# Gating step of an SSD stage on another engine, its stores on another queue, and other numbers of tile places

## The chip, the cores and the metric

The kernel runs on one core of a Trainium2 chip. A core has five engines that each work through their own list of instructions in order and meet through semaphores: TensorE (PE, matrix products), VectorE (DVE), ScalarE (ACT), GpSimd (POOL) and SyncE (SP, which here issues nearly all DMAs). The metric is the time of one execution on the device, in microseconds, and the figure for a kernel is the median of several executions.

## What is computed

The reference is an encoder trunk of two layers over 1024 tokens of width 1024. The even layer feeds two head groups from one input projection: A is a bidirectional state-space scan (SSD) with an output gate, B is a short gated convolution. The odd layer has latent attention and a multi-scale pooling. Cut to what the change touches:

```python
proj = x @ w_in
z, xbc, dt_raw, sc_bg, sc_cg, sc_h, sc_gate = split(proj)
xbc = silu(depthwise_conv(xbc, conv_w) + conv_b)
xs, bm, cm = split(xbc)
y_a = ssd_bidirectional(xs, bm, cm, dt_raw, a_log, dt_bias, d_skip)   # 16 heads, 4 groups, chunks of 128
y_a = rms_norm(y_a * silu(z), norm_g)
y_b = sc_bg * depthwise_conv(sc_cg * sc_h, sc_conv_w) * silu(sc_gate)
h = concatenate([y_a, y_b]) @ w_out
x = layer_norm(ALPHA * x + h)
```

The line that matters is `y_a * silu(z)`: the scan's output times the gate, whose squares are also summed for the norm.

## The kernel before

All products in float32 are made of three or six passes over pairs of a high and a low part. Layer 0 (`layer0_main`) runs in stages: a front stage projects x, B and C and convolves them (to about 230 us of the profile), the SSD stage computes the scan (about 230 to 600 us), a back stage finishes branch B and starts the output projection (from 600 us on); layer 1 follows.

The SSD stage loops over four groups of heads. For each group it runs over eight chunks twice. In the first pass, `op_p2` takes a chunk's x and B by TensorE transposes to `xps`, ScalarE copies x out (L743), a high and low part of B are made (`bhl`), x is scaled by dt into `xd` (VectorE, L751) and split into `xdh` (ScalarE) and `xdl` (GpSimd); `op_p2s` makes the chunk's state `sps` and adds it to the running states. For groups 1 to 3, `op_z` between them computes the gate's projection `zps` by 24 matmuls a chunk. ScalarE makes `zt`, a tanh (L724), and VectorE the gate `zs` from both (L725); only then is the `zps` place free. `zps` comes from a PSUM pool of two places, which it shares with `gps`, the products of branch B. In the trace `zs` is called ssd.

In the second pass, `op_p3f` loads `E`, decay rows of 512 KB spread over the partitions (L804), and works on them with ScalarE (L809, L810, L813) and VectorE (L811, L816 to L818); `op_p3b` makes the state part `yo` and the diagonal part in `cbp` (L836) on TensorE, moves yo out as `to` (VectorE, L834), adds up in `ta` on GpSimd (L838, L840) and VectorE (L841), multiplies by the gate into `yg` (L843), squares it on ScalarE with a sum into the norm (L844; the square's output overwrites `ta`) and stores `yg` to memory as yad (L845). At the end of a group `op_xl` loads the next group's four x, B and C tiles (L619).

The order of the program is that of `main_plan`: it also deals steps of branch B's products (`gps`) between the chunks, so that TensorE has other work. A scheduler of the framework then sets each engine's order within that. Tiles come from pools; tiles of one tag share a number of places, and a new tile waits until the last reader of the tile that stood in its place is done, a store included. Tag t1 (256 columns, four places) holds `bhl`, `hm`, `zt`, `ta` and `yg`. Tag t2 (512 columns, six places) holds the x tiles `xd`, `xdh`, `xdl` and also `to`. Tag cv (three places after the front stage) holds `brt` of branch B and in the back stage tiles of its Strassen-like combinations (L921, L997, L1002, L1004). `E` has four places.

Of the kernel before, what the change touches and what calls it, by code (L numbers as in the profile page):

```python
# [9 lines left out]
F32 = mybir.dt.float32  # L10
# [3 lines left out]
ALU = mybir.AluOpType  # L14
# [4 lines left out]
P = 128  # L19
# [52 lines left out]
YB_AT = (0, 1, 2, 3, 4, 5, 6, 7)  # L72
X_AT = (10, 11, 12, 13)
WOB, WOI, WOG, PI, NV, LA = 2, 3, 1, 1, 0, 2
T4B, T2B, CVB, RAWB, E2B = 1, 6, 3, 3, 4


def main_plan():
# [175 lines left out]
def bc_last(ap, n):  # L254
    s = list(ap.shape)
    return ap.unsqueeze(len(s)).broadcast_to(s + [n])
# [81 lines left out]
def view(t, n):  # L338
    return t.rearrange("p (a b) -> p a b", a=n)
# [166 lines left out]
def layer0_main(k):  # L506
    nc, tc, a = k.nc, k.tc, k.a
    V, A, GP, PE = nc.vector, nc.scalar, nc.gpsimd, nc.tensor
# [60 lines left out]
    tp = eb4 = dw4 = ecs4 = et4 = dt4 = ed4 = None  # L569
# [56 lines left out]
    def t2(name, dt=F32):  # L626
        return tp.tile([P, 512], dt, name=name, tag="t2", bufs=T2B)
# [2 lines left out]
        return (fp or cvp).tile([P, 512], F32, name=name, tag="cv", bufs=2 if fp is not None else CVB)  # L630

    def t1(name, dt=F32):
        return tp.tile([P, 256], dt, name=name, tag="t1", bufs=4)

    groups = [dict() for _ in range(G)]

# [79 lines left out]
    def op_z(g, c):  # L716
        st = groups[g]
        h, o = c // 4, (c % 4) * P
        ps = k.pa.tile([P, 1024], F32, name="zps", tag="pa")[:, 0:256]
        for kk in range(KD):  # L720
            wh, wl = st["zw"][kk // 4]
            mm3(nc, ps, *(t[:, o:o + P] for t in xhl(h, kk)), view(wh, 4)[:, kk % 4, :], view(wl, 4)[:, kk % 4, :], kk == 0, kk == KD - 1)
        zt = t1("zt")
        A.activation(out=zt, in_=ps, func=AF.Tanh, scale=0.5)  # L724
        V.scalar_tensor_tensor(out=st["zs"][:, c, :], in0=zt, scalar=1.0, in1=ps, op0=ALU.add, op1=ALU.mult)  # L725
# [4 lines left out]
    def h_cols(c):  # L730
        return slice(256 if c == 0 else 0, 256 if c == NB - 1 else 512)

    def dirs(cols):
        return slice(cols.start // 256, cols.stop // 256)

    def op_p2(g, c):
        st = groups[g]
        g4 = slice(4 * g, 4 * g + 4)
        hin = st["hin"]
        ps = k.pb.tile([P, 512], F32, name="xps", tag="pb")  # L740
        for j in range(3):
            st["xp"] = PE.transpose(out=ps[:, P * j:P * j + P], in_=st["xfm"][j][:, P * c:P * c + P], identity=k.ident).ins
        A.copy(out=st["xtm"][:, c, :], in_=ps[:, 0:256])  # L743
        bhl = t1("bhl", F32R)
        bh, bl = bhl[:, 0:P], bhl[:, P:256]
        split(nc, bh, bl, ps[:, 256:384], V)
        xd = t2("xd")
        xv = view(ps[:, 0:256], HPG)
        cols = s_cols(c)
        d = dirs(cols)  # L750
        V.tensor_tensor(out=xd.rearrange("p (q h d) -> p q h d", q=2, h=HPG)[:, d], in0=bc_mid(xv, 1, d.stop - d.start), in1=bc_last(dw4[:, c, d, g4], HD), op=ALU.mult)  # L751
        xh, xl = t2("xdh", F32R), t2("xdl", F32R)
        st["xa", c] = split(nc, xh[:, cols], xl[:, cols], xd[:, cols], nc.gpsimd)
        st["s", c] = (bh, bl, xh[:, cols], xl[:, cols])
# [23 lines left out]
    def h_decay(g, c, d):  # L778
        o = 256 * d
        hm = t1("hm")  # L780
        GP.tensor_tensor(out=view(hm, HPG), in0=view(groups[g]["hin"][:, c, o:o + 256], HPG), in1=bc_last(et4[:, c, d, 4 * g:4 * g + 4], HD), op=ALU.mult)
        return hm
# [39 lines left out]
    def op_p3b(g, c):  # L822
        st = groups[g]
        M, yd = st.pop(("f", c))
        g4 = slice(4 * g, 4 * g + 4)
        blk = slice(P * c, P * c + P)
        xt = st["xtm"][:, c, :]
        yo = k.pb.tile([P, 512], F32, name="yo", tag="pb")
        cols = h_cols(c)
        d = dirs(cols)  # L830
        PE.matmul(yo[:, cols], st["xfm"][3][:, blk], st["hin"][:, c, cols], start=True, stop=True)
        to = t2("to")
        tov, yov = (t.rearrange("p (d h e) -> p d h e", d=2, h=HPG)[:, d] for t in (to, yo))
        V.tensor_tensor(out=tov, in0=yov, in1=bc_last(ecs4[:, c, d, g4], HD), op=ALU.mult)  # L834
        for h in range(HPG):
            st["yd"] = PE.matmul(yd[:, HD * h:HD * h + HD], M[:, P * h:P * h + P], xt[:, HD * h:HD * h + HD], start=True, stop=True).ins  # L836
        ta = t1("ta")
        GP.tensor_tensor(out=view(ta, HPG), in0=view(xt, HPG), in1=bc_last(st.pop(("cd", c)), HD), op=ALU.mult)  # L838
        for q in range(d.start, d.stop):
            GP.tensor_tensor(out=ta, in0=to[:, 256 * q:256 * q + 256], in1=ta, op=ALU.add)  # L840
        V.tensor_tensor(out=ta, in0=yd, in1=ta, op=ALU.add)  # L841
        yg = t1("yg")
        GP.tensor_tensor(out=yg, in0=ta, in1=st["zs"][:, c, :], op=ALU.mult)  # L843
        A.activation(out=ta, in_=yg, func=AF.Square, accum_out=k.ssq[:, c, g:g + 1])  # L844
        nc.sync.dma_start(out=k.yad[c, :, 256 * g:256 * g + 256], in_=yg)  # L845

    def op_end():
        r = k.const.tile([P, NB], F32, name="rinv")
# [169 lines left out]
    def op_ya(c):  # L1018
# [10 lines left out]
        split(nc, t[:, 0, :, o:o + P], t[:, 1, :, o:o + P], view(y, KD), V)  # L1029

    table = {"fm": op_fm, "hold": op_hold, "dt2": op_dt2, "zx": op_zx, "ssd": op_ssd, "xl": op_xl, "z0": op_z0, "z": op_z, "p2": op_p2, "p2s": op_p2s, "p2b": op_p2b, "p3f": op_p3f, "p3b": op_p3b, "dt": op_dt, "end": op_end, "ya": op_ya, "tp": op_tp, "sw": op_sw, "sp": op_sp}
    for op in main_plan():
        table[op[0]](*op[1:])
# [606 lines left out]
```

## Time and profile before

| what | value |
| --- | --- |
| median of three runs (lowest to highest) | 1454.23 us (1453.46 to 1458.45) |
| the profiled execution | 1449.7 us |
| its span, first to last instruction | 1447.9 us |
| mean granted clock of TensorE | 0.983 |
| busy: TensorE, VectorE, ScalarE, GpSimd | 1391.6, 921.2, 692.1, 467.6 us |
| DMA, mean rate over the span | 101 GB/s |

Busy time is time in which an engine carries out an instruction; issuing a DMA or waiting doesn't count. A view of windows gives the same for a stretch of the span, with the clock that TensorE was granted as a share of its full speed (1.00 is 2.4 GHz, 0.50 is 1.2 GHz). A view of waits adds up the idle time of an engine before its instructions by what released it. A timeline lists instructions with their start, their length and, in brackets, the idle time before them and its releaser. A view of a tile lists all instructions that read or write it.

### The profile page before, as it was taken

What the parts mean: (1) busy time and instruction counts of PE and PEld (TensorE: products, weight loads), DVE (VectorE), ACT (ScalarE), POOL (GpSimd) and SP (SyncE); (2) the same over time, 40 slices, a digit from 0 to 9 for tenths busy, and PEclk for the clock granted to TensorE, in tenths of its full rate; (3) what the DMA queues carried; (4) which work ended last, traced back from release to release, by engine and by line L of the source; (5) the groups of instructions that cost most, each with busy time, mean ns of one, the idle gap of its engine ahead of it and who ended that gap; (6) DMA issues with size and microseconds to landing.
All of it is one profiled execution on the core that took longest, in us unless ns stands there. A gap on an engine that the chain in (4) does not pass through costs nothing.

```text
span 1447.9 us, 19653 instructions
## 1 busy us (share of the span) xinstructions
PE 1391.6 (96%) x7215; PEld 1183.1 (82%) x7215; DVE 921.2 (64%) x1564; ACT 692.1 (48%) x1350; POOL 467.6 (32%) x452
## 2 busy tenths in 40 slices
PE   8999999998989797999999999999999999999997
PEld 7878888787879685788888888898888888988886
DVE  5787886465555657667577443733235888888485
ACT  5254554555546555343235232522224788888510
POOL 0021220355444546423210060612320355556211
PEclk9999999999999999899999999999999999999999
DMA  7332236454451515332247455201100000001232
GB/s 253 119 101 102 104 115 242 151 117 116 124 168 60 170 35 130 117 100 86 82 150 225 173 166 202 95 31 58 41 26 1 1 1 1 1 30 59 87 117 87
DMA packets 55520, 146.40 MB, mean 101 GB/s; under 512 B 6264, under 2 KB 11648, under 8 KB 55296
## 3 DMA queue, kind: packets, MB, share of 16 engines
q1 hardware_dynamic: 55424, 145.15, 32.0%
q8 instruction: 57, 0.93, 0.3%
q14 instruction: 39, 0.32, 0.1%
HBM read 118.78 MB, written 26.35 MB: 100 GB/s over the span
## 4 chain that ended last, share of the span: by engine, by line
PE 76%; DMA 8%; DVE 8%; ACT 4%; issue 2%; POOL 2%; SPq 0%; DVEq 0%; POOLq 0%; ACTq 0%
PE sA L953 10%; PE sD L953 5%; PE ops L424 4%; PE ops L425 4%; PE ops L427 4%; PE tps L1462 3%; PE fps L418 3%; PE fps L417 3%; PE fps L419 3%; DMA E<-crow 2%; PE gps L424 2%; PE gps L425 2%; PE gps L427 2%; PE sps L417 2%; PE sB L953 2%; PE sps L418 2%
## 5 line engine op out<-in xcount | busy, mean ns | idle before, releaser
L424 PE MATMUL gps<-x,whi 128*128 128x512 f32 x320 | 129.1, 404 | 0.4 <-ACT bru L672 0.2
L425 PE MATMUL gps<-x,whi 128*128 128x512 f32 x320 | 127.7, 399 | 0.0
L499 DVE TENSOR_TENSOR wlo<-wraw,whi 128x1024 fp32r<-128x1024 f32 x54 | 70.0, 1296 | 62.8 <-ACT whi L498 62.7
L1448 POOL TENSOR_SCALAR pt<-pt,sm 128x1024 f32<-128x1024 f32 x64 | 72.8, 1138 | 114.4 <-DVE sm L1447 63.4
L427 PE MATMUL gps<-x,wlo 128*128 128x512 f32 x320 | 102.6, 400 | 0.1
L498 ACT CAST whi<-wraw 128x1024 fp32r<-128x1024 f32 x54 | 56.7, 1050 | 94.2 <-PE ops L427 43.4
L902 POOL TENSOR_TENSOR s3t<-sraw 128x512 f32<-128x512 f32 x14 | 22.3, 1594 | 230.0 <-DMA sraw<-in_wt_dram 192.4
L499 DVE TENSOR_TENSOR PT<-tps,PT 128x512 fp32r<-128x512 f32 x128 | 84.2, 682 | 12.6 <-ACT PT L498 12.3
L1442 DVE TENSOR_REDUCE nm<-sps 128x1 f32<-128x1024 f32 x64 | 77.9, 1218 | 9.5 <-PE sps L419 9.3
L1056 POOL TENSOR_TENSOR rs<-rs,neghalf 128x1 f32<-128x1 f32 x16 | 12.9, 812 | 211.5 <-DVE nm L1091 143.8
L1446 ACT ACTIVATE pt<-sps,nm 128x1024 f32<-128x1024 f32 x64 | 71.8, 1122 | 17.4 <-DVE nm L1443 14.2
L498 ACT CAST PT<-tps 128x512 fp32r<-128x512 f32 x128 | 70.0, 588 | 16.1 <-PE tps L1462 15.6
L417 PE MATMUL zps<-whi,x 128*128 128x256 f32 x192 | 58.8, 306 | 16.8 <-DVE ssd L725 16.8
L417 PE MATMUL fps<-x1hi,whi 128*128 128x512 f32 x192 | 74.9, 390 | 0.0
L419 PE MATMUL fps<-x1hi,wlo 128*128 128x512 f32 x192 | 74.7, 389 | 0.0
L418 PE MATMUL fps<-x1lo,whi 128*128 128x512 f32 x192 | 74.7, 389 | 0.0
L424 PEld LDWEIGHTS gps<-x,whi 128*128 128x128 f32 x320 | 61.2, 191 | 13.9 <-issue 0.7
L427 PEld LDWEIGHTS gps<-x,wlo 128*128 128x128 f32 x320 | 60.8, 190 | 14.1 <-issue 1.0
L425 PEld LDWEIGHTS gps<-x,whi 128*128 128x128 f32 x320 | 61.2, 191 | 12.6 <-issue 0.7
L1462 PE MATMUL tps<-consts,pt 128*128 128x128 f32 x512 | 70.2, 273 | 0.3 <-DVE PT L499 0.3
L499 POOL TENSOR_TENSOR xdl<-xd,xdh 128x512 fp32r<-128x512 f32 (+1 forms) x32 | 38.4, 1205 | 98.5 <-ACT xdh L498 97.4
L646 DVE SCALAR_TENSOR_TENSOR cacc<-u,vec,cacc 128x1023 f32<-128x1023 f32 (+1 forms) x48 | 65.8, 1386 | 3.2 <-ACT cacc L643 3.0
(377 smaller groups left out, 4218.3 us busy)
## 6 DMA issues: line engine op xcount, KB each, us to landing
wraw<-in_wt_dram SPq DMA_DIRECT2D x70, 512.0 KB, 4.3
E<-crow SPq DMA_DIRECT2D x32, 512.0 KB, 6.2
sraw<-in_wt_dram SPq DMA_DIRECT2D x28, 512.0 KB, 3.7
xtraw<-in_xT_dram SPq DMA_DIRECT2D x16, 512.0 KB, 4.0
xbd<-cacc SPq DMA_DIRECT2D x16, 512.0 KB, 2.6
ssd<-xbd SPq DMA_DIRECT2D x16, 512.0 KB, 5.3
ybd<-bra SPq DMA_DIRECT2D x16, 256.0 KB, 2.7
yad<-yg SPq DMA_DIRECT2D x32, 128.0 KB, 3.1
```

Source lines behind the costliest of these rows:

```text
L417: nc.tensor.matmul(out, shi, mhi, start=start, stop=False)
L418: nc.tensor.matmul(out, shi, mlo, start=False, stop=False)
L419: nc.tensor.matmul(out, slo, mhi, start=False, stop=stop)
L424: nc.tensor.matmul(out, shi, mhi, start=start, stop=False)
L425: nc.tensor.matmul(out, shi, mlo, start=False, stop=False)
L427: nc.tensor.matmul(out, slo, mhi, start=False, stop=stop)
L498: cast = nc.scalar.copy(out=hi, in_=src)
L499: lo_eng.tensor_tensor(out=lo, in0=src, in1=hi.bitcast(F32), op=ALU.subtract)
L953: st["last"] = PE.matmul(ps, s_[:, kk, :], x_, start=fresh and kk == 0 and m == 0, stop=kk == 3 and m == 2, skip_group_check=True).ins
L1442: V.tensor_reduce(out=nm, in_=ps, axis=AX.X, op=ALU.max)
L1448: GP.tensor_scalar(out=pt, in0=pt, scalar1=sm, scalar2=1.0, op0=ALU.mult, op1=ALU.mult)
L1462: PE.transpose(out=ps[:, P * c:P * c + P], in_=pt[:, P * (4 * h + c):P * (4 * h + c) + P], identity=k.ident)
```

## The change

The gating multiply (L843) moves from GpSimd to VectorE. Its output yg gets a tag of its own with three places instead of a place of t1. The store of yg (L845) is issued by ScalarE instead of SyncE, 32 times in all. Tag t1 gets five places instead of four, tag t2 five instead of six, and tag cv two instead of three.

```diff
-T4B, T2B, CVB, RAWB, E2B = 1, 6, 3, 3, 4
+T1B, T4B, T2B, CVB, RAWB, E2B = 5, 1, 5, 2, 3, 4
...
     def t1(name, dt=F32):
-        return tp.tile([P, 256], dt, name=name, tag="t1", bufs=4)
+        return tp.tile([P, 256], dt, name=name, tag="t1", bufs=T1B)
...
         V.tensor_tensor(out=ta, in0=yd, in1=ta, op=ALU.add)
-        yg = t1("yg")
-        GP.tensor_tensor(out=yg, in0=ta, in1=st["zs"][:, c, :], op=ALU.mult)
+        yg = tp.tile([P, 256], F32, name="yg", tag="yg", bufs=3)
+        V.tensor_tensor(out=yg, in0=ta, in1=st["zs"][:, c, :], op=ALU.mult)
         A.activation(out=ta, in_=yg, func=AF.Square, accum_out=k.ssq[:, c, g:g + 1])
-        nc.sync.dma_start(out=k.yad[c, :, 256 * g:256 * g + 256], in_=yg)
+        A.dma_start(out=k.yad[c, :, 256 * g:256 * g + 256], in_=yg)
```

The scheduler orders the engines anew. The rows below show an engine's instructions in their order, with line, operation, output and inputs, and in brackets the semaphores that the instruction waits for; DMAHW is one of eight semaphores of landed DMAs.

ScalarE where group 1 ends and group 2 begins, before:

```order
L844 ACTIVATE ta,ssq<-yg 128x256 [waits DMAHW1_49,DMAHW7_49,Activation_49,Pool_49]
L844 ACTIVATE ta,ssq<-yg 128x256 [waits Activation_49,Pool_49]
L743 COPY ssd_1886<-xps 128x256 [waits PE_49] x2
L498 CAST bhl<-xps 128x128 [waits Activation_49]
L724 ACTIVATE zt<-zps 128x256 [waits DMAHW2_49,DMAHW1_49,DMAHW0_49]
L844 ACTIVATE ta,ssq<-yg 128x256 [waits Pool_49]
L498 CAST xdh<-xd 128x256 [waits DVE_49]
```

The same place after the change:

```order
L844 ACTIVATE ta,ssq<-yg 128x256 [waits DVE_49,Pool_49]
L845 DMA yad<-yg 128x256
L813 ACTIVATE E_3538<-E_3538,dtx 128x128 [waits DVE_49]
L813 ACTIVATE E_3538<-E_3538,dtx 128x128 x3
L743 COPY ssd_1886<-xps 128x256 [waits PE_49]
L498 CAST bhl<-xps 128x128 [waits Activation_49]
L724 ACTIVATE zt<-zps 128x256 [waits Activation_49]
L844 ACTIVATE ta,ssq<-yg 128x256 [waits DVE_49,Pool_49]
L845 DMA yad<-yg 128x256 [waits DMAHW0_49]
```

The new group's first zt stands one square and one copy further ahead and waits for no DMA; a store stands behind each square, some with a DMA's semaphore.

VectorE where group 2 ends and group 3 begins, before:

```order
L834 TENSOR_TENSOR to<-yo,ecs 128x512 [waits PE_49]
L841 TENSOR_TENSOR ta<-cbp,ta 128x256 [waits Pool_49]
L841 TENSOR_TENSOR ta<-cbp,ta 128x256 [waits PE_49,Activation_49,Pool_49]
L499 TENSOR_TENSOR bhl<-xps,bhl 128x128 [waits Activation_49]
L751 TENSOR_TENSOR xd<-xps,dw 128x256
L725 SCALAR_TENSOR_TENSOR ssd_1888<-zt,zps 128x256 [waits Activation_49]
```

The same place after the change:

```order
L834 TENSOR_TENSOR to<-yo,ecs 128x512 [waits PE_49]
L841 TENSOR_TENSOR ta<-cbp,ta 128x256 [waits Pool_49]
L499 TENSOR_TENSOR bhl<-xps,bhl 128x128 [waits PE_49,Activation_49]
L751 TENSOR_TENSOR xd<-xps,dw 128x256
L725 SCALAR_TENSOR_TENSOR ssd_1888<-zt,zps 128x256 [waits Activation_49]
L843 TENSOR_TENSOR yg<-ta,ssd_1888 128x256 [waits DMAHW0_49,DVE_49]
L499 TENSOR_TENSOR bhl<-xps,bhl 128x128 [waits PE_49,Activation_49]
L841 TENSOR_TENSOR ta<-cbp,ta 128x256 [waits Pool_49]
```

The last ta now stands behind the first gate step L725, and the gating multiplies stand between, each with the semaphore of an earlier store.

SyncE near the end of group 3, before:

```order
L687 DMA ybd<-bra 128x512 [waits DMAHW7_49,Pool_49]
L804 DMA E_5125<-crow 128x2x512 [waits DMAHW0_49,PE_49]
L845 DMA yad<-yg 128x256 [waits Pool_49]
L687 DMA ybd<-bra 128x512 [waits Pool_49]
L845 DMA yad<-yg 128x256 [waits DMAHW3_49,Pool_49]
L804 DMA E_5180<-crow 128x2x512 [waits DMAHW4_49,DVE_49,PE_49]
L804 DMA E_5228<-crow 128x2x512 [waits DMAHW5_49,DVE_49,PE_49]
L845 DMA yad<-yg 128x256 [waits DMAHW6_49,Pool_49]
```

The same place after the change:

```order
L804 DMA E_5125<-crow 128x2x512 [waits DMAHW7_49,PE_49]
L687 DMA ybd<-bra 128x512 [waits DMAHW0_49,Pool_49]
L687 DMA ybd<-bra 128x512 [waits Pool_49]
L804 DMA E_5180<-crow 128x2x512 [waits DMAHW4_49,DVE_49,PE_49]
L804 DMA E_5228<-crow 128x2x512 [waits DMAHW6_49,DVE_49,PE_49]
```

The loads of E_5125, E_5180 and E_5228, the last three of the stage, have no store of yg ahead of them any more, and E_5125 also stands ahead of a store of bra.

## Rows read from the trace of the kernel before

**Rows 1.** The page: busy time (share) and instructions; a costly group, busy and mean ns.

```profile
PE 1391.6 (96%) x7215; PEld 1183.1 (82%) x7215; DVE 921.2 (64%) x1564; ACT 692.1 (48%) x1350; POOL 467.6 (32%) x452
...
L499 POOL TENSOR_TENSOR xdl<-xd,xdh 128x512 fp32r<-128x512 f32 (+1 forms) x32 | 38.4, 1205 | 98.5 <-ACT xdh L498 97.4
```

**Rows 2.** Windows: stretch, its length, busy PE, PEld, DVE, ACT, POOL; clock, DMA share, GB/s.

```profile
340.00:360.00 20.00, 16.50 (x118) 16.15 (x119) 7.63 (x20) 10.00 (x32) 9.32 (x12) 0.83 0.17 44
420.00:440.00 20.00, 14.61 (x111) 14.34 (x111) 5.96 (x16) 7.13 (x24) 8.57 (x11) 0.83 0.46 149
500.00:520.00 20.00, 12.38 (x92) 11.98 (x92) 6.30 (x18) 7.48 (x25) 9.54 (x13) 0.83 0.34 73
560.00:600.00 40.00, 32.21 (x126) 24.71 (x125) 25.05 (x51) 20.15 (x61) 21.84 (x26) 0.79 0.46 126
600.00:800.00 200.00, 198.81 (x905) 163.59 (x904) 131.25 (x176) 78.24 (x102) 42.59 (x29) 1.00 0.42 131
```

**Rows 3.** Waits of TensorE from 230 to 620: us in total, times, longest.

```profile
PE zps L417 <- DVE ssd L725: 16.8, 3, 7.6
PE yo L831 <- DVE to L834: 5.1, 2, 4.8
PE sps L417 <- ACT xdh L498: 2.4, 1, 2.4
PE yo L831 <- DVE ta L841: 2.1, 1, 2.1
```

**Rows 4.** Timeline at the joints of the groups: start, us, instruction [idle before, releaser].

```profile
343.50 0.58 PE L417 MATMUL zps<-whi,x 128*128 128x256 f32 x1 [3.74 <-DVE ssd L725]
...
422.24 0.35 ACT L743 COPY ssd<-xps 128x256 f32<-128x256 f32 x1
...
429.49 0.58 PE L417 MATMUL zps<-whi,x 128*128 128x256 f32 x1 [5.39 <-DVE ssd L725]
...
499.94 0.35 ACT L743 COPY ssd<-xps 128x256 f32<-128x256 f32 x1
...
507.66 0.38 ACT L724 ACTIVATE zt<-zps 128x256 f32<-128x256 f32 x1 [3.89 <-DMA yad<-yg]
...
508.55 0.58 PE L417 MATMUL zps<-whi,x 128*128 128x256 f32 x1 [7.62 <-DVE ssd L725]
```

**Rows 5.** The tile yg: ns least/median/most, first and last start; landing of its stores.

```profile
L843 POOL TENSOR_TENSOR yg<-ta,ssd x32: 722/734/1650, 307.1 to 593.0; 128x256 f32<-128x256 f32 x32
L845 SPq DMA_DIRECT2D yad<-yg x32: 319/330/614, 307.8 to 594.7; - x32
...
DMA to landing us min/median/max: 1.7/3.1/7.9
```

**Rows 6.** Waits of SyncE's queue, GpSimd and ScalarE from 230 to 620.

```profile
SPq L845 <- POOL yg L843: 77.2, 30, 6.0
...
POOL yg L843 <- DVE ta L841: 32.2, 29, 3.3
...
ACT zt L724 <- DMA yad<-yg: 8.8, 2, 4.9
```

**Rows 7.** Timeline near the end of group 3.

```profile
563.79 1.27 ACT L809 ACTIVATE E<-E,ed 128x128 f32<-128x128 f32 x4 [2.17 <-DMA E<-crow]
...
566.82 1.22 PE L831 MATMUL yo<-ssd,ssd 128*128 128x256 f32 x2 [4.78 <-DVE to L834]
```

**Rows 8.** Windows of 2 us of TensorE: busy, clock, DMA share, GB/s.

```profile
339.00:341.00 2.00, 0.55 (x3) 0.94 0.64 256
425.00:427.00 2.00, 0.00 (x0) 0.77 1.08 365
503.00:505.00 2.00, 0.00 (x0) 0.90 1.03 236
```

**Rows 9.** The tile ta: ns least/median/most, first and last start.

```profile
L840 POOL TENSOR_TENSOR ta<-to,ta x56: 721/731/1817, 304.8 to 589.9; 128x256 f32<-128x256 f32 x56
L841 DVE TENSOR_TENSOR ta<-cbp,ta x32: 408/425/428, 306.6 to 592.6; 128x256 f32<-128x256 f32 x32
```

## The prediction

> **What bounds the kernel now.** I read the share of busy time first. TensorE is busy 96% of the span [rows 1], so only what shortens TensorE's idle time, or the time that it runs slowly, can shorten the kernel. The windows by stage come next, because a share over the whole span hides where the idle time lies: the reader should see full windows in the gated back stage (198.81 of 200 us from 600 on) and holes at four places of the SSD stage, at the joints after groups 0, 1 and 2 (16.50, 14.61 and 12.38 of 20 us) and at the end of group 3 (32.21 of 40) [rows 2]. The waits of TensorE name them: 16.8 us in three waits of the z product for VectorE's gate step L725, then 5.1 us and 2.1 us of the state product yo for VectorE [rows 3]. I call these joints T1, T2, T3 and the end T4.
>
> What makes L725 late stands in the timeline. At T3 ScalarE's zt waited 3.89 us for the store yad<-yg, VectorE followed, and TensorE went on at 508.55 after 7.62 us; at T2 it was 5.39 us, at T1 3.74 us [rows 4]. So the first zt of a group stands still because it needs a t1 place that a gated output still holds until its store has landed, and the z product has two PSUM places, which only zt and L725 empty. A store takes 3.1 us to land in the median and up to 7.9 [rows 5]. The other queues agree: SP stands 77.2 us at the stores for GpSimd, GpSimd stands 32.2 us at yg for VectorE, and ScalarE stands 8.8 us at two zt for the store [rows 6]. T4 is of another kind: ScalarE waits 2.17 us for an E load, and yo follows 4.78 us late [rows 7], and 2.1 us late once more [rows 3].
>
> A hole costs twice. The granted clock falls to its lower level within about two microseconds of the start of each hole: slices that begin at full clock average 0.94, 0.77 and 0.90 [rows 8], which puts the falls at 340.8, 426.1 and 504.6 us. The 20 us slices average 0.83 [rows 2], so the clock was halved for 6.8 us in each; after the idle part that leaves 4.1, 3.4 and 2.9 us of work at half speed, and half of that is lost: 2.0, 1.7 and 1.4 us. For T4 the mean is 0.79 over 40 us, so 16.8 us at half clock, of which at most the 7.8 idle ones did no work: 4.5 to 8.4 us are lost.
>
> **The change, part by part.** *T2 and T3, places.* yg leaves the tag t1 for three places of its own and t1 gets five. The first zt of a group then waits for no store: its semaphores are ScalarE's own. The order on the engines agrees: zt moves ahead of the last gating multiplies and their squares, and L725 ahead of the last chunk's ta. In the new order zt follows the copy L743 of the group's first chunk and one short cast. At T2 that copy ends at 422.6 [rows 4], so zt can start near 423 and L725 near 423.4, before TensorE has used up its second PSUM place at 424.1 (429.49 less 5.39): the whole 5.39 us go and with them 1.7 us of clock, 7.1. At T3 the copy ends at 500.3, L725 can end near 501.6, and TensorE stood from 500.9, so some 0.7 us of the 7.62 stay: 6.9 + 1.4 = 8.3. What is late next is the chain bhl, xd, xdh, xdl to the state product; TensorE waited 2.4 us there once in the stage [rows 3], and I take off 1.5 us for the two joints. Sum 14, bounds 7 (each hole keeps half) and 15.4.
>
> *T1.* The idle 3.74 us end with VectorE, which in the new order has two gating multiplies ahead of the first L725 that it hadn't before. Bounds: a loss of 1 us (two multiplies) and 5.7 (hole and clock go). I take 1.5, close to the lower end, because VectorE's own work ends there and no store is waited for.
>
> *T4, SP's queue.* The 32 stores leave SP's queue, in which an E load that is ready stands behind a store that waits for GpSimd. At the end of group 3 the load of the third-last E tile also moves ahead of a store of bra that waits for GpSimd. Its place is free once the products of four chunks earlier are done; the next load follows with it. Of the 6.9 us of idle time [rows 3, 7] I take 3, and 1 us of clock: 4. Bounds 0 (the load, not the queue, is what takes long) and 6.9 + 8.4 = 15.3.
>
> The Trainium skill, "DMA: Bandwidth & Descriptors", section "Issuing engines are not separate DMA queues", says that all engines' transfers share the same 16 DMA engines and that another issuing engine only saves the issuing time. By that rule T4 would bring nothing and the forecast would be 4 us higher; the 77.2 us that SP stands at the stores [rows 6] speak for more than that, since a queue in order holds back what is behind.
>
> *VectorE's 32 gating multiplies.* The nearest rows are L841 at 425 ns with one input in PSUM, and GpSimd's 734 ns for the same step [rows 5, 9]: 13.6 to 23.5 us of VectorE. Through T1 to T3 VectorE is busy 6.0 to 7.6 of 20 us, at T4 25 of 40 [rows 2], so this lies beside other work, and the handover GpSimd to VectorE to GpSimd becomes one step on VectorE. What stands behind: the multiply waits for the landing of the store three chunks earlier, and with it all of VectorE. At 3.4 us a chunk that store has some 10 us, more than the longest 7.9 [rows 5]. Cost 0, bounds -1 and 12 (about 0.4 us a chunk, if VectorE paces the chunks).
>
> *ScalarE's 32 issues.* SP's issue took 0.33 us [rows 5]; the trace has no DMA issued by ScalarE, so 0 to 0.33 us each, 0 to 10.6 us, right behind a square that waited for yg anyway. Some also wait for an older transfer's landing; these were issued long before. I take 0 at TensorE, 3 at worst.
>
> *GpSimd* loses 32 x 0.73 = 23.5 us and its waits for VectorE. That shortens the chain of ta at the joints, which the terms above include.
>
> *One x place fewer.* With five t2 places eight of the 32 xd steps wait for a state product or for a subtract on GpSimd just before (1.2 us each [rows 1]) that they hadn't to wait for. TensorE is covered there by z products and fillers. I take 1.5 us, bounds 0 and 8 x 1.2 = 9.6.
>
> *Two cv places instead of three.* This touches the back stage, where VectorE is busy 131 of 200 us and TensorE 198.81 [rows 2]; TensorE's buffered work covers it. I take 0.5 us, bounds 0 and 4 (three extra waits of about 1.2 us).
>
> *Sum*: 14 + 1.5 + 4 - 1.5 - 0.5 = 17.5, and 1.5 us off for what the trace can't show at the joints: 16 us. TensorE is full after 600, so nothing there takes this back. The profiled run took 1449.7 us, 4.5 below the median of the three timed runs, 1454.2. From the profiled run the sum gives 1433.7, from the median 1438; I forecast the median.
>
> **The rivals.** *The end gains too (B).* T4 closes almost wholly: 8 us more, 1430. For it: a shorter chain of ta and E loads that no store holds. Against it: an E load takes its time to land whatever the queue before it, and E tiles still have four places.
>
> *The wait only moves (C).* VectorE, in order, is now what the joint waits for: the L841 in front of the first L725 waits for GpSimd's adds, and half of T2 and T3 stays. The gain falls to about 5 us: 1449. For it: T1 was VectorE's already. Against it: in the new order L725 stands ahead of the last ta.
>
> *Slower: the two engines shut each other out (D).* The multiply now reads two SBUF tiles on VectorE while GpSimd adds ta. L840 took 731 ns in the median and up to 1817, and yg up to 1650 [rows 5, 9], so something does stretch GpSimd's steps by about 1.1 us. If each of the 32 multiplies and the step of GpSimd beside it are stretched by half of that, 0.55 us each on the one chain of a chunk, 1.1 x 32 = 35 us are added; about two thirds lie beside other work, some 10 us come to TensorE, and the holes at T2 and T3 stay as they were: of the gain of 16 us 14 go, and 10 more, so 1462. It decides from the point where a stretched chunk is longer than TensorE's work for it. Against it: GpSimd loses 0.73 us a chunk, and most L840 took the plain 731 ns though VectorE was busy half the time. The Trainium skill, "SBUF — State Buffer", section "Who interferes with whom", states such a rule: VectorE with two SBUF inputs and GpSimd reading SBUF exclude each other. The longest steps agree with it, the median doesn't need it.
>
> **How the numbers follow.** Chances: forecast (A) 0.60, B 0.13, C 0.16, D 0.11. A's own range is 1430 to 1447. The range for all reaches down into B and up past C: 1427 to 1455; below lies half of B at most and above lies D with a little of C. Half a percent is 7.3 us, about what a measurement of this kernel can tell from no change; faster means below 1447. A gives 0.58 of that and B 0.13, C 0.05: 0.76. Same: 0.02 of A, 0.10 of C, 0.01 of D: 0.13. Slower: 0.01 of C and 0.10 of D: 0.11.
>
> **What would show it.** In the profile of the changed kernel: no wait of zps for L725 above 1 us at T2 and T3, TensorE's busy time there above 18 of 20 us and the clock full; no zt that waits for yad<-yg; at T1 still 2 to 3 us; at T4 two waits of yo that sum to about 4 us. D would show as gating multiplies near 1 us and L840 with a median well above 731 ns. My working is wrong if VectorE's gating multiply waits long for yad<-yg, if ScalarE stands at the stores, or if sps waits for xdl in every group.

## The result and the profile after

The changed kernel takes 1432.16 us in the median (1429.78 to 1436.67), the kernel before 1453.85 beside it: a ratio of 0.9851 with a 95% interval of 0.9824 to 0.9879, some 22 us less. Run once more on the chip of the last experiments it took 1434.22 us, ratio 0.9868 (0.9851 to 0.9885). The profiled execution took 1432.96 us with a span of 1431.1, 16.8 us below the span of before; the median gained more than this pair of executions, so the lines below explain about 17 of the 22 us, and the rest is spread between executions.

The windows of the changed kernel (columns as in [rows 2]):

```profile
340.00:360.00 20.00, 19.36 (x153) 18.77 (x154) 8.47 (x22) 13.56 (x44) 9.31 (x11) 1.00 0.23 78
...
420.00:440.00 20.00, 20.00 (x161) 19.32 (x160) 8.03 (x20) 13.61 (x44) 8.05 (x9) 1.00 0.17 35
440.00:500.00 60.00, 56.29 (x330) 47.51 (x329) 44.70 (x100) 32.90 (x101) 27.82 (x36) 0.97 0.47 140
500.00:520.00 20.00, 20.00 (x141) 18.50 (x140) 10.34 (x19) 13.65 (x39) 9.84 (x10) 1.00 0.09 27
520.00:560.00 40.00, 36.92 (x160) 28.79 (x159) 33.22 (x71) 21.30 (x64) 23.43 (x26) 0.86 0.50 132
560.00:600.00 40.00, 37.43 (x144) 28.85 (x143) 28.89 (x43) 16.82 (x31) 9.05 (x8) 0.85 0.35 105
```

The stage runs earlier now, by 3 us at its first joint and by 22 at its end, so windows don't cover the same work, but the holes can be found again: T1 and T2 are nearly or wholly closed and the clock stays at its full level there; T3 now lies in 440 to 500; and the end of group 3, in 520 to 600, still loses 5.65 us of idle time and 0.14 to 0.15 of the clock.

TensorE's waits from 230 to 620 say the same (columns as in [rows 3]):

```profile
PE yo L831 <- DVE to L834: 2.8, 2, 2.0
PE cbp L801 <- DVE ta L841: 2.7, 2, 2.2
PE sps L417 <- ACT xdh L498: 2.4, 1, 2.4
PE sA L953 <- ACT whi L498: 2.3, 1, 2.3
PE zps L417 <- DVE ssd L725: 1.9, 2, 1.4
```

The z product waited 16.8 us before [rows 3] and 1.9 us now. The wait of sA, the first product of the back stage, for its weights has grown, from 0.5 us to 2.3. The timeline of TensorE has the places (columns as in [rows 4]):

```profile
340.64 0.39 PE L417 MATMUL zps<-whi,x 128*128 128x256 f32 x1 [1.40 <-DVE ssd L725]
...
484.78 0.49 PE L801 MATMUL cbp<-ssd 128*128 128x128 f32 x2 [2.23 <-DVE ta L841]
...
492.58 0.38 PE L417 MATMUL zps<-whi,x 128*128 128x256 f32 x1 [0.47 <-DVE ssd L725]
...
592.17 0.73 PE L953 MATMUL sA<-x,whi 128*128 128x512 f32 x2 [2.26 <-ACT whi L498]
```

T1 has 1.40 us left of 3.74, T2 nothing of 5.39, T3 0.47 of 7.62 [rows 4]. But in the second pass of group 2 a wait of 2.23 us for VectorE's ta is larger than any there before (1.20 us in that pass).

The tile yg, and L840 from the view of ta (columns as in [rows 5, 9]):

```profile
L843 DVE TENSOR_TENSOR yg<-ta,ssd x32: 409/426/1133, 307.6 to 570.4; 128x256 f32<-128x256 f32 x32
L845 ACTq DMA_DIRECT2D yad<-yg x32: 326/326/345, 309.7 to 571.0; - x32
...
DMA to landing us min/median/max: 1.7/4.0/7.5
```

```profile
L840 POOL TENSOR_TENSOR ta<-to,ta x56: 720/736/1595, 305.6 to 567.0; 128x256 f32<-128x256 f32 x56
```

The multiply takes 426 ns on VectorE instead of 734 on GpSimd [rows 5], and GpSimd's adds stay at 736 (731 before [rows 9]). No wait of zt, of VectorE or of ScalarE for yad<-yg is left in the stage.

### The profile page after: what moved, and what is told of

Read it like the earlier page. It is cut to its first block, busy times and chain, and to the rows that moved or that the text cites. A ratio compares the mean times of both kernels' runs of the same rounds, so it can differ in the third digit from the quotient of the medians.

```text
span 1431.1 us, 19645 instructions
## 1 busy us (share of the span) xinstructions
PE 1392.4 (97%) x7215; PEld 1182.2 (83%) x7215; DVE 936.3 (65%) x1596; ACT 692.3 (48%) x1350; POOL 443.5 (31%) x420
## 4 chain that ended last, share of the span: by engine, by line
PE 69%; DVE 6%; DMA 3%; ACT 2%; issue 1%; POOL 0%; ACTq 0%; DVEq 0%
PE sA L953 5%; PE ops L427 4%; PE ops L425 4%; PE ops L424 4%; PE tps L1462 3%; PE fps L417 3%; PE fps L418 3%; PE fps L419 3%; PE sps L417 2%; PE sD L953 2%; PE sps L418 2%; PE sps L419 2%; PE gps L424 2%; PE gps L425 2%; PE gps L427 2%; PE o1ps L427 2%
## 5 line engine op out<-in xcount | busy, mean ns | idle before, releaser
L1477 PE MATMUL yps<-PT,vv 128*128 128x256 f32 x256 | 65.7, 286 | 0.0
```

## The experiments

The title of the change names an engine and a queue; the numbers of places come last. Two theories stood at the start. P: the joints' gain is that of the places. Q: it is that of the shorter chain on GpSimd and the freed queue of SyncE. The first four runs take the change apart.

**New numbers alone.** The changed kernel with multiply and store put back:

```diff
-        V.tensor_tensor(out=yg, in0=ta, in1=st["zs"][:, c, :], op=ALU.mult)
+        GP.tensor_tensor(out=yg, in0=ta, in1=st["zs"][:, c, :], op=ALU.mult)
...
-        A.dma_start(out=k.yad[c, :, 256 * g:256 * g + 256], in_=yg)
+        nc.sync.dma_start(out=k.yad[c, :, 256 * g:256 * g + 256], in_=yg)
```

> The new numbers of places alone: yg has three places of its own, t1 five, t2 five, cv two, but GpSimd still multiplies and SyncE still stores. Theory P (the joints stood because zt had to wait for a place that a gated output held): the z product's waits for L725 fall from 16.8 us to under 4 us at groups 1 to 2 and 2 to 3, and the kernel takes about 14 us less than before, 1438 to 1443. Rival Q (the gain comes from the shorter chain on GpSimd and the freed queue of SyncE): 1450 or more.

Measured: 1428.49 us (1427.68 to 1429.96), ratio 0.9833 (0.9812 to 0.9854). That is the whole gain, and 10 us more gain than P had expected. Its waits of TensorE:

```profile
PE sA L953 <- ACT whi L498: 3.2, 1, 3.2
PE yo L831 <- DVE to L834: 2.6, 2, 2.3
...
PE zps L417 <- DVE ssd L725: 1.7, 2, 1.3
```

**New engine and queue alone.** The kernel before with these two lines changed:

```diff
-        GP.tensor_tensor(out=yg, in0=ta, in1=st["zs"][:, c, :], op=ALU.mult)
+        V.tensor_tensor(out=yg, in0=ta, in1=st["zs"][:, c, :], op=ALU.mult)
...
-        nc.sync.dma_start(out=k.yad[c, :, 256 * g:256 * g + 256], in_=yg)
+        A.dma_start(out=k.yad[c, :, 256 * g:256 * g + 256], in_=yg)
```

> The new engine and the new queue alone: VectorE multiplies, ScalarE stores, with the places of before (yg from t1's four, t2 six, cv three). P: the first zt of a group still waits for a store, which now stands right ahead of it in ScalarE's list, so nothing is gained at the joints and only the end of group 3 is shorter: 1449 to 1460. Q: most of the gain, 1436 to 1442.

Measured: 1452.67 us (1447.12 to 1455.89), ratio 0.9992 (0.9976 to 1.0007): nothing. The z product's waits fell from 16.8 us to 12.5, but those of the state product for ScalarE's xdh rose from 2.4 to 6.0. T3 in its timeline, ScalarE and then TensorE:

```profile
511.46 0.38 ACT L724 ACTIVATE zt<-zps 128x256 f32<-128x256 f32 x1 [4.25 <-DMA yad<-yg]
```

```profile
512.35 0.58 PE L417 MATMUL zps<-whi,x 128*128 128x256 f32 x1 [7.37 <-DVE ssd L725]
```

The store now leaves from ScalarE's own list, and zt behind it still waits for it to land: 7.37 us of TensorE against 7.62 [rows 4]. Q has fallen.

**Store back on SyncE; multiply back on GpSimd.** Two runs, each the changed kernel with one of the two lines of the first diff.

> The changed kernel with the stores issued by SyncE again. P: 0 to 5 us above the changed kernel, and the difference lies after 540 us, where loads of E stand behind stores: 1432 to 1437. Q: 8 us or more above the changed kernel.

> The changed kernel with the gating multiply on GpSimd again, stores on ScalarE's queue. P: GpSimd's chain of a chunk is longer by one step of 0.73 us and a handover, seen at the end of group 3 and a little at the joints: 2 to 6 us above the changed kernel, 1434 to 1438. Q: 10 us or more above it.

Measured: with the store back 1434.50 us (1433.51 to 1435.36), ratio 0.9871 (0.9853 to 0.9889); with the multiply back 1430.21 us (1427.93 to 1431.59), ratio 0.9840 (0.9820 to 0.9860). The second is a miss of P as well: I had expected 2 to 6 us more than the changed kernel, and it took no more. On one chip, next to the new numbers alone (1428.5), the multiply on VectorE costs 6.0 us with the stores on SyncE, with no overlap of the runs; the store on ScalarE's queue costs 1.7, within the scatter. With the stores on ScalarE the multiply costs less: the changed kernel's 1432.16 lies 2.0 above 1430.21, and the runs overlap. P had put the price of SyncE's stores after 540 us; it is not there (see T4 below).

Where the multiply on VectorE costs is seen in the second pass of group 2. The same waits, first with the new numbers alone, then with the multiply on VectorE and the store on SyncE, from 440 to 500:

```profile
PE cbp L801 <- DVE ta L841: 1.0, 1, 1.0
...
PE yo L831 <- DVE to L834: 0.3, 1, 0.3
```

```profile
PE cbp L801 <- DVE ta L841: 2.0, 1, 2.0
...
PE yo L831 <- DVE to L834: 0.8, 1, 0.8
```

TensorE waits for ta and to, and VectorE comes to them later; the granted clock of that window is 1.00 in the first kernel and 0.94 in the second, which is 7.2 of 60 us at half clock. So 1.5 us more wait and up to 3.6 us of slower work lie here; the rest of the 6 us is not placed.

That the multiply can stay on GpSimd at no cost shows in GpSimd's waits, of the new numbers alone and of the run with eight shared places below:

```profile
POOL yg L843 <- DVE ta L841: 6.7, 8, 2.9
```

```profile
POOL yg L843 <- DVE ta L841: 35.7, 30, 3.5
```

With places of its own yg is put off: GpSimd adds up the next chunk's ta while VectorE finishes this one's, and waits 8 times instead of 29 [rows 6]. The handover that the multiply on VectorE saves was then no longer waited for.

**Number or separation?** The new theory S says that zt must not stand in line behind a store; the rival N that t1 was too small. The first of the next four runs has yg in t1 with all eight places together, t2 five and cv two; against the new numbers alone its edit is:

```diff
-T1B, T4B, T2B, CVB, RAWB, E2B = 5, 1, 5, 2, 3, 4
+T1B, T4B, T2B, CVB, RAWB, E2B = 8, 1, 5, 2, 3, 4
...
-        yg = tp.tile([P, 256], F32, name="yg", tag="yg", bufs=3)
+        yg = t1("yg")
```

> As the run with the new numbers alone (GpSimd multiplies, SyncE stores, t2 five, cv two), but yg stays in tag t1, which gets eight places: as many for both as five and three apart. Theory S (what counts is that a zt never stands in line behind a store): the places are handed on in turn, zt still gets the place of an earlier yg, and waits of zt for yad<-yg with holes at groups 1 to 2 and 2 to 3 come back: 1440 to 1455. Rival N (the number of places counts): 1427 to 1432, like the run with the new numbers.

Measured: 1443.75 us (1440.12 to 1443.96), ratio 0.9923 (0.9896 to 0.9951). More places help, by some 10 us; separate ones give 13 to 15 more (1430.7 with two places for yg, below, and 1428.49 with three). Its waits of TensorE at T2 and T3:

```profile
426.12 0.39 PE L417 MATMUL zps<-whi,x 128*128 128x256 f32 x1 [1.23 <-DVE ssd L725]
...
501.02 0.58 PE L417 MATMUL zps<-whi,x 128*128 128x256 f32 x1 [4.86 <-DVE ssd L725]
```

S is right in the time, but these holes do not show its reason. At T3 ScalarE's first zt, at 498.07, waited for no store. The second did, for 1.59 us, but the hole ended with the first L725 at 500.56, and VectorE came to that one straight from the last ta, for which it had stood 3.01 us for GpSimd's adds: the order of before. T2 is alike, with 2.44 us for the last ta. With its own places for yg the scheduler puts L725 ahead of that ta. So separate places do two things: zt waits for no store, and VectorE's order changes. With the first zt free and the old order, T1 keeps 3.74 us, T2 1.23 and T3 4.86, that is 9.8 of the 16.8 us. The kernel before shows the two one behind the other at T3:

```profile
505.13 0.42 DVE L841 TENSOR_TENSOR ta<-cbp,ta 128x256 f32<-128x256 f32 x1 [3.01 <-POOL ta L840]
...
508.08 0.42 DVE L725 SCALAR_TENSOR_TENSOR ssd<-zt,zps 128x256 f32<-128x256 f32 x1 [1.99 <-ACT zt L724]
```

Of the 7.62 us there, VectorE stood only the last 1.99 us for the zt that waited for a store; at T2 it was 4.05 of 5.39.

**Which memory is taken.** Two runs with yg in two places and t1 at four as before; the memory comes from cv alone (t2 six, cv two) or from t2 alone (t2 five, cv three). The edit of the first, against the new numbers alone; the second has 4, 1, 5, 3, 3, 4:

```diff
-T1B, T4B, T2B, CVB, RAWB, E2B = 5, 1, 5, 2, 3, 4
+T1B, T4B, T2B, CVB, RAWB, E2B = 4, 1, 6, 2, 3, 4
...
-        yg = tp.tile([P, 256], F32, name="yg", tag="yg", bufs=3)
+        yg = tp.tile([P, 256], F32, name="yg", tag="yg", bufs=2)
```

> yg in two places of its own, t1 four as before, t2 six as before, cv two: the memory comes from cv alone. GpSimd multiplies, SyncE stores. S: zt waits for no store, so 1426 to 1434; with two places yg may wait for its own store, up to 3 us. N: t1 with four places is as tight as before, 1440 or more.

> yg in two places of its own, t1 four, t2 five, cv three as before: the memory comes from t2 alone. S: 1427 to 1436; against the run that takes it from cv the difference is the price of the t2 place less that of the cv place, 0 to 3 us by my sum (1.5 and 0.5). N: 1440 or more.

Measured: 1430.72 us (1429.71 to 1431.31), ratio 0.9839, and 1430.76 us (1428.72 to 1434.53), ratio 0.9843. t1 needs no fifth place and yg no third, and which tag gives makes no difference beyond the scatter.

**The places taken, and nothing given.** The kernel before with t2 five and cv two:

```diff
-T4B, T2B, CVB, RAWB, E2B = 1, 6, 3, 3, 4
+T4B, T2B, CVB, RAWB, E2B = 1, 5, 2, 3, 4
```

> The kernel before with t2 five and cv two and nothing given in return: the price of the places taken. By my sum 2 us slower than before, 1452 to 1462; if the x tiles do not need the sixth place, no change.

Measured: 1454.15 us, ratio 1.0000 (0.9986 to 1.0014). The places taken cost nothing, to within 2 us.

**zt apart instead of yg.** The kernel before with one other tile given its own tag, and cv at two:

```diff
-        zt = t1("zt")
+        zt = tp.tile([P, 256], F32, name="zt", tag="zt", bufs=2)
```

> The kernel before, with only zt taken out of tag t1, into two places of its own (cv two); yg stays in t1 and everything else as before. Theory S in its wide form (whatever shares places with yg inherits its store's landing, and holds up all that stands behind it in its engine's list): bhl of the new group, a t1 tile as well, now waits for the stores, with the second zt behind it on ScalarE; the first zt passes, so the holes at groups 1 to 2 and 2 to 3 shrink by about the 2.9 us of one more z product each but stay: 1440 to 1449. The narrow form (zt's own wait is all): 1430 to 1437 as with yg apart.

Measured: 1446.78 us (1445.18 to 1447.89), ratio 0.9957 (0.9941 to 0.9973). The time is that of the wide form, but the holes are smaller than it said. ScalarE at T2, and then TensorE's waits from 230 to 620:

```profile
424.39 0.27 ACT L498 CAST bhl<-xps 128x128 fp32r<-128x128 f32 x1 [4.69 <-DMA yad<-yg]
424.56 0.39 ACT L724 ACTIVATE zt<-zps 128x256 f32<-128x256 f32 x1
```

```profile
PE cbp L836 <- DVE E L818: 7.3, 3, 5.6
PE sA L953 <- ACT whi L498: 5.7, 1, 5.7
...
PE zps L417 <- DVE ssd L725: 1.5, 1, 1.5
```

The wait for the store went to bhl, the other t1 tile, with the group's third zt behind it; two had passed, at 413.54 and 415.37. The z product lost only 1.5 us. That the two zt which pass give TensorE enough work to cover the rest is my reading; VectorE's order is another one here too. The 15 us that the z product no longer waits are mostly lost elsewhere: 5.6 us near the end of the stage, 5.7 before sA, and the state product waits 7.1 us for xdh and xdl instead of 2.9. What stays is the second pass of group 3. Its eight L841, before, here, with the new numbers alone, and with the new engine and queue alone:

```profile
L841 DVE TENSOR_TENSOR ta<-cbp,ta x8: 410/420/428, 555.5 to 592.6; 128x256 f32<-128x256 f32 x8
```

```profile
L841 DVE TENSOR_TENSOR ta<-cbp,ta x8: 406/416/426, 549.0 to 585.8; 128x256 f32<-128x256 f32 x8
```

```profile
L841 DVE TENSOR_TENSOR ta<-cbp,ta x8: 411/414/425, 537.8 to 565.3; 128x256 f32<-128x256 f32 x8
```

```profile
L841 DVE TENSOR_TENSOR ta<-cbp,ta x8: 410/416/425, 562.6 to 593.4; 128x256 f32<-128x256 f32 x8
```

From the first L841 to the last it takes 37.1 us before and 36.9 here, 27.5 with places for yg, and 30.9 with the new engine and queue. So closing the z product's holes is not enough, and neither is a shorter second pass: the run with the new engine and queue has that and gains nothing.

**What could still be had.** Two more runs start from the new numbers alone (GpSimd multiplies, SyncE stores). The first deals one more step of branch B's products to each chunk of group 3; the second also plans the last transposed x tiles of the back stage earlier:

```diff
-F2, F3, FB, FX = (2, 0, 0, 0), (3, 3, 2, 2), 0, 8
+F2, F3, FB, FX = (2, 0, 0, 0), (3, 3, 2, 3), 0, 8
```

```diff
     ops.append(("tp", 2))
-    pull(4)
     ops.append(("tp", 3))
-    pull(4)
+    pull(8)
```

With them on the same chip the changed kernel ran once more:

> The changed kernel once more, on the chip of the other runs of this call: 1429 to 1435. Beside the next two runs it gives the price of VectorE's multiply and ScalarE's stores on the same chip.

> The new numbers alone (GpSimd multiplies, SyncE stores), and eight more steps of branch B's products dealt into group 3, one a chunk, taken from those that run after the stage. If the holes left at the end of group 3 (2.3, 0.5 and 1.5 us and 40 us at a clock of 0.79) are all that is left there, TensorE fills them: 1421 to 1426. If the chain of loads that starts the back stage (the wait of 3.2 us before sA) sets the end, nothing is gained, 1427 to 1432, and that wait grows by what was saved.

> As the run before, and the last transposed x tiles of the back stage (the step tp 3) planned ahead of four product steps instead of behind them, so that its loads and with them the first weights of the back stage come earlier. If the chain of loads sets the end: 3 to 5 us below the run before. If not: the same within 2 us.

Measured: the changed kernel 1434.22 us (1431.70 to 1434.53); more fillers 1422.26 us (1420.42 to 1424.30), ratio 0.9786 (0.9764 to 0.9808); with the earlier tiles 1420.45 us (1416.90 to 1421.24), ratio 0.9772 (0.9753 to 0.9791). Both beat both kernels. Windows of the new numbers alone, and then of more fillers:

```profile
520.00:560.00 40.00, 35.51 (x144) 26.62 (x143) 31.61 (x70) 22.00 (x71) 26.46 (x32) 0.79 0.49 124
560.00:600.00 40.00, 36.77 (x161) 29.83 (x160) 26.92 (x35) 14.98 (x20) 10.78 (x9) 0.95 0.41 128
```

```profile
520.00:560.00 40.00, 38.77 (x189) 31.01 (x187) 31.36 (x59) 18.88 (x53) 22.26 (x24) 1.00 0.58 153
560.00:600.00 40.00, 37.56 (x173) 30.11 (x173) 31.14 (x50) 19.20 (x43) 16.63 (x19) 1.00 0.35 110
```

TensorE is busy 3.3 us more in the first window and the clock stays at its full level in both. The wait of the first sA for its weights is gone, so the chain of loads did not set the end. Against the new numbers alone (1428.49, on another chip) that is 6 us more. The second run's further 1.8 us are within the scatter: whether the earlier tiles help stays open.

## Why the prediction was right, point by point

- **T2 and T3** (forecast 14 us after a deduction): right in mechanism and nearly in size. Of 13.01 us of holes 0.47 are left, and the clock is full from 340 to 440 and from 500 to 520. The deduction of 1.5 us was for the chain bhl, xd, xdh, xdl; no such wait came behind a joint. What came instead lies in the second pass of group 2: 2.23 us and 0.81 us of TensorE for VectorE's ta and to. Two readings were off. The prediction laid these holes to the store; at T3 VectorE stood only 1.99 of the 7.62 us for it, and before that for GpSimd's adds, which the new order passes by as well. And the clock did not fall within about two microseconds of each hole's start: at T3 it was 3.7 us (504.6 less 500.9).
- **T1** (forecast 1.5): the term was mis-sized. The hole fell by 2.34 us and the clock, 2.0 us by my working, no longer fell (0.83 before, 1.00 now from 340 to 360): 4.3. I had put the two gating multiplies ahead of L725 and nothing else. But VectorE stood 2.41 us for GpSimd's adds of the last ta before, with L725 behind it at 343.04; now L725 stands ahead of that ta, at 340.18. This too comes with the places: with them alone it came at 338.64 us, with the new engine and queue alone at 347.50.
- **T4, SyncE's queue** (forecast 4): the time came, by another cause. From the first L725 of group 3 to the end of the stage (L849) it took 87.2 us before and 81.1 after. Two pairs of runs differ in the queue alone: 81.1 with the stores on ScalarE and 80.5 on SyncE where VectorE multiplies, 79.6 and 80.6 where GpSimd does. So the queue is worth no more than 1 us here, either way. All four have the new places; the new engine and queue without them took 84.6. (The first L725 moves with the order, so the measure fits only runs of like order: with zt apart it gives 108.3.) What in the new order shortens the stretch is not shown. The loads that I thought the stores held back move with it. SyncE's issues of the E loads near the end, with the new engine and queue alone and with the places alone:

```profile
558.02 0.39 SPq L804 DMA_DIRECT2D E<-crow  x1
...
565.70 9.40 SPq L804 DMA_DIRECT2D E<-crow  x2
```

```profile
529.29 1.26 SPq L804 DMA_DIRECT2D E<-crow  x2
...
542.24 0.37 SPq L804 DMA_DIRECT2D E<-crow  x1
...
549.69 0.37 SPq L804 DMA_DIRECT2D E<-crow  x1
```

  In the second, the loads of the fourth-last and third-last E tile stand side by side, with no store of bra between them as in the first (at 557.59), though the queue carries all 32 stores of yg. The rule that the prediction quoted from the Trainium skill, "DMA: Bandwidth & Descriptors", section "Issuing engines are not separate DMA queues", says that another issuing engine only saves the issuing time. The runs agree with it: 1.7 us more beside the new numbers alone. My argument from the 77.2 us of SyncE [rows 6] was wrong: with the places alone the queue stands nearly as long, and the whole gain is there.

```profile
SPq L845 <- POOL yg L843: 72.2, 31, 6.8
```

  A queue that waits has to be shown to hold back something that is late.
- **VectorE's multiplies and ScalarE's issues** (forecast 0, bounds -1 and 12): the price of the multiply was 6.0 us with the stores on SyncE and 2.0, within the scatter, with those on ScalarE. It lay within the bounds, but the row I took it from, 425 ns beside other work, says nothing of the order: VectorE does its list in turn, and ta and to came later.
- **The places taken** (forecast 2 us): 0, to within 2.
- **Back stage** (forecast: nothing is taken back): wrong. From L849 to the first sA it took 14.8 us before and 18.9 after, and sA waited 2.26 us for its weights. About 4 us of the gain in the stage, 22.0 us at L849, were given back there; at the end of the span 16.8 are left. With the new numbers alone it is 18.9 us as well, with more fillers 10.1; what else holds the start of the back stage the runs do not separate.
- **The rivals.** B (the end gains too) came in part: T4 gained 6 us instead of 4. C did not come here; its mechanism, L725 behind a ta that waits for GpSimd, is what eight shared places left. D did not come in the time, but its mechanism did. The prediction quoted for it the Trainium skill, "SBUF — State Buffer", section "Who interferes with whom", by which VectorE with two SBUF inputs and GpSimd reading SBUF exclude each other. The trace agrees: 13 of the 32 multiplies began while GpSimd was inside an instruction with 0.20 us or more to go. Each of them ended 0.28 us after that instruction and took 476 to 1133 ns; the other 19 took 409 to 427. L841, with one input in PSUM, began beside such an instruction five times and took 408 to 425 ns. The changed kernel's second profile has 13 stretched multiplies as well. One of each, GpSimd first:

```profile
318.07 0.62 POOL L838 TENSOR_TENSOR ta<-ssd,cd 128x256 f32<-128x256 f32 x1 [1.20 <-DVE cd L817]
...
318.11 0.86 DVE L843 TENSOR_TENSOR yg<-ta,ssd 128x256 f32<-128x256 f32 x1
```

```profile
382.56 0.61 POOL L838 TENSOR_TENSOR ta<-ssd,cd 128x256 f32<-128x256 f32 x1
382.64 0.42 DVE L841 TENSOR_TENSOR ta<-cbp,ta 128x256 f32<-128x256 f32 x1 [0.64 <-POOL ta L840]
```

  In sum the 13 are stretched by 3.6 us, where D had put 0.55 us on each of the 32; the median of 426 ns hides it. How much of it reached TensorE is not shown. L840's longest, 1595 ns, is no sign of it: it was 1817 before [rows 9].

In sum, between the two profiled executions, the stage gained 22.0 us where I had forecast 16, and 5.2 us were given back after it, 4.1 before sA and 1.1 to the end of the span, where I had forecast nothing: 16.8 are left, and 22 in the medians. The direction and the main mechanism held, that of the places. That the profiled pair came within 1 us of the forecast gain is luck: 6 us too little in the stage and 5.2 us forgotten behind it cancel. And two of the three things that the title names, the other engine and the other queue, were not the cause; without the experiments the time would have seemed to confirm them.

## What to carry to other kernels

A tile that is released only when a store has landed is worth trying with places of its own: in a shared tag it passed its landing time on to whatever tile came next in that tag (zt, or bhl once zt was apart), and the engine's order passed that on again. Look at the new order as well as at the wait, since the scheduler changes it with the tags; here the order was worth as much at the joints as the store. Test the parts of such a change one by one: places alone gave the whole gain, the engine and the queue alone nothing. A wait of a queue or an engine, however long, is worth nothing until something on the path is seen to be late because of it, and work that covers the last stage of a pipeline (here eight product steps moved) was worth another quarter of the gain.

## What was not expected of the hardware

The issue of a store from ScalarE took 326 ns, but it did not keep ScalarE from its next activation. In the changed kernel a square L844 starts at 339.82, the issue beside it at 339.87, and the next activation at 340.29, 0.47 us behind the square:

```profile
339.82 0.42 ACT L844 ACTIVATE ta<-yg 128x256 f32<-128x256 f32 x1
339.87 0.33 ACTq L845 DMA_DIRECT2D yad<-yg  x1
...
340.29 0.41 ACT L498 CAST xdh<-xd 128x256 fp32r<-128x256 f32 x1
```

Where the next activation followed at once, it started 0.40 to 0.53 us behind the square, 13 times; in the kernel before, with no issue there, 0.40 to 0.54 us, 17 times.

The stores landed later from there, 4.0 us in the median against 3.1 [rows 5]. With the multiply on GpSimd and the store on ScalarE it was 3.8, with the multiply on VectorE and the store on SyncE 2.8. So it goes with the queue in these runs; why it does, none of them shows.
